# Two encoder layers on one core: the front of the first layer rebuilt

## The chip, the core and the metric

The kernel runs on one core of a Trainium2 chip. The metric is the device time of one execution in microseconds, the median over runs; three runs of the kernel before took 3671.44, 3666.75 and 3673.9 us. The core's engines are TensorE (PE; its weight loads are listed as PEld), VectorE (DVE), ScalarE (ACT), GpSimd (POOL) and SyncE (SP, which issues most DMAs). Each works through its own list of instructions in order and waits on semaphores for the others.

## What is computed

The reference is a trunk of two layers over 1024 tokens of width 1024, in float32. The first layer mixes tokens by multi-head latent attention, the second by dilated windows; both end in an MLP. Only the first layer's start matters here:

```python
cond = jax.nn.silu(c)
mod = (cond @ ada_w[i] + ada_b[i]).reshape(B, N_MOD, D)        # shift1, scale1, gate1, shift2, ...
h = rms_norm(x, norm_mix[i]) * (1 + scale1) + shift1
proj = h @ w_in                                                # 384 + 256 + 32 columns
q_lat, kv_lat = proj[..., :384], proj[..., 384:640]
k_rope = rope(proj[..., 640:], pos)
q = (rms_norm(q_lat, g_qa) @ w_qb).reshape(B, S, 16, 96)       # 64 plain + 32 rotated per head
kv = (rms_norm(kv_lat, g_kva) @ w_kvb).reshape(B, S, 16, 128)  # 64 of k, 64 of v per head
q = rms_norm(rotated q, g_q);  k = rms_norm(k with k_rope, g_k)
o = softmax(q k^T / sqrt(96)) v;  y = o @ w_o;  x = x + gate1 * y
```

The positions are an input. The second layer's bias depends on them; where they are evenly spaced (they are here) a short way to the bias table is taken, else a long one under a branch.

## The kernel before

Every large product is made of three float32r matmuls: both operands are split into a high part and the rest, and high x high, high x rest and rest x high are summed in PSUM (`mm3`, lines 289 to 293). A split (`split`, 114) is a copy on ACT and a subtraction on DVE. Tiles live in SBUF pools of 4 KB slots: `G` has 29 slots for the whole program, `X` 16 slots from `aux()` on. The instructions of each engine are ordered by a planner that simulates the program, so the order of the source is kept where nothing is won by another; an instruction passed to `keep_in_program_order` keeps its place among the others so marked.

**Start (lines 1383 to 1407).** SP loads four tiles of x, the constants (`const_loads`, 119) and the first half of the modulation weights of scale1 and shift1. `bias_check` (796) loads the positions into one partition and tests on DVE, over 1023 elements, whether they are even. `consts` (133) makes `cond`. Four tiles of x are normalised together (`xhat`, 234), transposed on PE and kept (`xT`). For each half of the 1024 columns the modulation sum is made on DVE, eight multiply-adds of 512 columns for each of the two (`ada_sum`, 167), and summed over partitions by matmuls with a column of ones (`ada_end`, 177, line 192). Then h is written, transposed, as h high and h rest (`h_store`, 262). The branch on even positions (`bias_any`, 894, line 897) follows; every engine passes it together.

**First projection (`mla`, lines 411 to 452).** Eight tiles of 128 tokens are multiplied with w_in, 384 and 288 columns, all eight blocks of D one after the other for each tile; four tiles make a half. Each tile's latents are evicted and normalised (428 to 437), after four tiles they are transposed (444). Before each tile of the second half stand two modulation steps (420). `rope_tables` (315) makes sines and cosines on POOL and DVE.

**Heads (lines 470 to 520).** For two halves of the heads and eight tiles each, q (`pq`, two banks, two buffers) and k and v (`pkv`, the same) are projected; ACT and DVE sum squares, the factor of the norm is made (`rstd`, 99), DVE multiplies q (`tq`, 502) and k (505, 507), POOL rotates q (`rope`, 376) and multiplies it by the weights of both norms (512, 514), and `st` is stored to DRAM but for the first four heads (520).

**Attention (lines 523 to 652).** 64 units, each of two blocks of 128 queries, in a software pipeline: scores, minimum (575), exp (576), factor (579), transposes (590), product with v (603). `prep` (528) transposes and splits a head's q and k; that of head 0 stands before the loop. Every eleventh of the 269 turns has a modulation step (`ada_step`, 206), which sums 128 columns of a later modulation, by turns on DVE (eight operations, 173 and 175) and on POOL (four, 162 to 165).

Of the kernel before, what the change touches and what calls it, by code (L numbers as in the profile page):

```python
# [9 lines left out]
F32 = mybir.dt.float32  # L10
# [10 lines left out]
P = 128  # L21
# [20 lines left out]
class K:  # L42
# [76 lines left out]
    def const_loads(self):  # L119
        nc, a = self.nc, self.a  # L120
        rows = self.G("rows", [P, P], F32)
        nc.sync.dma_start(out=rows[0:96, :], in_=a["ada_b"].rearrange("l (r p) -> (l r) p", p=P))
        nc.sync.dma_start(out=rows[96:112, :], in_=a["norm_mix"].rearrange("l (r p) -> (l r) p", p=P))
        nc.sync.dma_start(out=rows[112:128, :], in_=a["norm_mlp"].rearrange("l (r p) -> (l r) p", p=P))
        rows2 = self.G("rows2", [P, P], F32)
        nc.sync.dma_start(out=rows2[0:3, :], in_=a["mla_g_qa"].rearrange("o (r p) -> (o r) p", p=P))
        nc.sync.dma_start(out=rows2[3:5, :], in_=a["mla_g_kva"].rearrange("o (r p) -> (o r) p", p=P))

        cc = self.C("cc", [P, 8])
        nc.sync.dma_start(out=cc, in_=a["c"].rearrange("o (p j) -> p (o j)", j=8))  # L130
        return rows, rows2, cc
# [17 lines left out]
    def ada_load(self, l, s, c, n, alloc=None):  # L149

        w = self.a["ada_w"][l].rearrange("(p j) n -> p j n", j=8)[:, :, s * 1024 + c : s * 1024 + c + n]
        if alloc is None:
            t = self.dap.tile([P, 8, n], F32, tag="w", name=self.nm("adaw"))
            self.nc.sync.dma_start(out=t, in_=w)
            return [t]
        m = 1024 // n
        return [self.load(w[:, j : j + m, :], (P, m, n), "adaw", alloc=alloc) for j in range(0, 8, m)]

    def ada_sum_pool(self, w, n, acc):

        tt = self.nc.gpsimd.tensor_tensor
        tt(w, w, self.cond.unsqueeze(2).broadcast_to([P, 8, n]), op=ALU.mult)
        tt(w[:, 0:4], w[:, 0:4], w[:, 4:8], op=ALU.add)
        tt(w[:, 0:2], w[:, 0:2], w[:, 2:4], op=ALU.add)
        tt(acc, w[:, 0], w[:, 1], op=ALU.add)

    def ada_sum(self, ws, n, acc):
        nc = self.nc
        m = 8 // len(ws)
        for j in range(8):  # L170
# [3 lines left out]
            else:  # L174
                nc.vector.scalar_tensor_tensor(acc, g, self.cond[:, j : j + 1], acc, op0=ALU.mult, op1=ALU.add)  # L175

    def ada_end(self, l, s, c, n, acc, psp, tag):
# [10 lines left out]
        if (l, s) not in self.mods:  # L188
            self.mods[(l, s)] = self.C(f"mod{l}{s}", [P, 8])
        d0, nd = c // P, n // P  # L190
        for d in range(nd):
            nc.tensor.matmul(ps[:, d : d + 1], acc[:, d * P : (d + 1) * P], self.ones[:, 0:1], start=True, stop=True)
        mo = self.mods[(l, s)][:, d0 : d0 + nd]
        b = l * 48 + s * 8 + d0
        nc.vector.tensor_tensor(mo, ps[:, 0:nd], self.colc[:, b : b + nd], op=ALU.add)
        if s % 3 == 1:
            b = (96 if s == 1 else 112) + l * 8 + d0
            nc.vector.scalar_tensor_tensor(mo, mo, 1.0, self.colc[:, b : b + nd], op0=ALU.add, op1=ALU.mult)
# [26 lines left out]
    def xhat1(self, x, alloc=None):  # L225
# [4 lines left out]
        nc.scalar.activation(g, x, AF.Square, scale=1.0 / 32.0, accum_out=ms)  # L230
# [45 lines left out]
    def h_steps(self, xs, mods, alloc=None, halloc=None, single=False):  # L276
# [4 lines left out]
        if single:  # L281
            steps = [lambda psp, tag, x=x: xh.append(self.xhat1(x, alloc)) for x in xs]
# [12 lines left out]
    def load(self, src, shape, name, dt=F32, alloc=None):  # L295
        g = (alloc or self.G)(name, shape, dt)
        self.nc.sync.dma_start(out=g, in_=src)
# [17 lines left out]
    def rope_tables(self):  # L315
        nc, a = self.nc, self.a
        eng = nc.gpsimd
        pos = self.M("posc", [P, 8], I32)
        nc.sync.dma_start(out=pos, in_=a["positions"].rearrange("o (t p) -> p (o t)", p=P))
        posf = self.M("posf", [P, 8])  # L320
        nc.vector.tensor_copy(posf, pos)
# [54 lines left out]
    def rope(self, eng, out, x, t, n, name):  # L376

        cos = self.cs["cos"][:, t : t + 1, :].broadcast_to([P, n, 16])
        sin = self.cs["sin"][:, t : t + 1, :].broadcast_to([P, n, 16])
        u = self.mp.tile([P, n, 16], F32, tag="rp", bufs=3, name=self.nm(name + "u"))  # L380
        w = self.mp.tile([P, n, 16], F32, tag="rp", bufs=3, name=self.nm(name + "w"))
        x1, x2 = x[:, :, 0:16], x[:, :, 16:32]
        eng.tensor_tensor(u, x1, cos, op=ALU.mult)
        eng.tensor_tensor(w, x2, sin, op=ALU.mult)
        eng.tensor_tensor(out[:, :, 0:16], u, w, op=ALU.subtract)
        u = self.mp.tile([P, n, 16], F32, tag="rp", bufs=3, name=self.nm(name + "u2"))
        w = self.mp.tile([P, n, 16], F32, tag="rp", bufs=3, name=self.nm(name + "w2"))
        eng.tensor_tensor(u, x2, cos, op=ALU.mult)
        eng.tensor_tensor(w, x1, sin, op=ALU.mult)
        eng.tensor_tensor(out[:, :, 16:32], u, w, op=ALU.add)  # L390


    def mla(self, at, wi, xs1, mods, tail):
# [9 lines left out]
        def heads_w(hf, alloc):  # L403
            wq = [self.wsplit(a["mla_w_qb"][0, c * P : (c + 1) * P, hf * 768 : (hf + 1) * 768], (P, 768), "wq",
                              gain=self.colc[:, 128 + c : 129 + c], alloc=alloc) for c in range(3)]
            wkv = [self.wsplit(a["mla_w_kvb"][0, c * P : (c + 1) * P, hf * 1024 : (hf + 1) * 1024], (P, 1024), "wkv",
                               gain=self.colc[:, 131 + c : 132 + c], alloc=alloc) for c in range(2)]
            return wq, wkv

        with tc.tile_pool(name="psA", bufs=2, space=PSUM, reuse_waits="tile") as psp:  # L410
            at1, steps = self.h_steps(xs1, mods, self.X, self.X)
            steps.pop(0)(psp, "b1")
            self.rope_tables()
            for half in range(2):
                lats = []
                h = (at, at1)[half]
                for t in range(half * 4, half * 4 + 4):
                    if half == 1:
                        for i in range(2):
                            self.ada_step(psp, "b1", i == 1)  # L420
                    tl = slice((t % 4) * P, (t % 4 + 1) * P)
                    ps = psp.tile([P, 2, 512], F32, tag="b2", name=self.nm("psin"))
                    for o, n, b in ((0, 384, 0), (384, 288, 1)):
                        for d in range(ND):
                            self.mm3(ps[:, b, 0:n], h(0, d)[:, tl], h(1, d)[:, tl],
                                     wi[d][0][:, o : o + n], wi[d][1][:, o : o + n], d == 0, d == ND - 1)
                    ms = self.sm("lms", 2)
                    lat = self.G("lat", (P, 640), F32)
                    nc.scalar.activation(lat[:, 0:384], ps[:, 0, 0:384], AF.Square, scale=QL ** -0.5,
                                         accum_out=ms[:, 0:1])  # L430
                    nc.scalar.activation(lat[:, 384:640], ps[:, 1, 0:256], AF.Square, scale=KL ** -0.5,
                                         accum_out=ms[:, 1:2])
                    r = self.rstd(ms, 2, "lr")
                    nc.vector.tensor_scalar(lat[:, 0:384], ps[:, 0, 0:384], r[:, 0:1], None, op0=ALU.mult)
                    nc.vector.tensor_scalar(lat[:, 384:640], ps[:, 1, 0:256], r[:, 1:2], None, op0=ALU.mult)
                    nc.vector.tensor_copy(krw[:, t, :], ps[:, 1, 256:288])
# [1080 lines left out]
```

## Time and profile before

| | us |
|---|---|
| median of three runs | 3671.44 |
| the profiled execution | 3669.05 |
| its span | 3667.3 |
| PE busy | 3493.4 |
| DVE busy | 2458.3 |
| ACT busy | 1482.0 |
| POOL busy | 960.6 |

The span is the time from the first instruction to the last of the profiled execution. An engine's busy time leaves out waits, branches and the issuing of DMAs. A row of a group names the line, the engine, the operation, the tile written and those read, the shape and the count, then the busy time, the mean duration of one in ns, and the idle time before them with what ended it. A row of the timeline begins with its start and its duration. A row of the stages gives busy time by engine, the clock that PE was granted (1.00 is full speed), the share of the DMA engines and GB/s.

### The profile page before, as it was taken

The numbers are of one execution on the slowest core, as the hardware profiler recorded it, in microseconds if no ns is written. First come the engines' busy times: TensorE is split into PE (matmuls) and PEld (weight loads), VectorE is DVE, ScalarE is ACT, GpSimd is POOL, SyncE is SP. The second block draws the span as 40 slices with busy tenths as digits, with TensorE's granted clock in tenths as the row PEclk, the third lists the DMA queues.
The fourth block names the chain that finished last, engine by engine and source line by source line (L and its number), as shares of the span: only waits on it lengthen the run. The fifth ranks groups of instructions, "written<-read, shape, count | busy, mean of one in ns | idle before, by whom it ended". The sixth has DMA issues, their size and how long they took to land.

```text
span 3667.3 us, 58438 instructions
## 1 busy us (share of the span) xinstructions
PE 3493.4 (95%) x22163; PEld 3109.7 (85%) x22163; DVE 2458.3 (67%) x5045; ACT 1482.0 (40%) x3133; POOL 960.6 (26%) x1323
## 2 busy tenths in 40 slices
PE   3799999999999999999999999999998899999999
PEld 3787788778888878889999999999998778888887
DVE  6788888767777775566667666676877565455554
ACT  3336777653211112235556454565555232112221
POOL 3476555530111111112222222233334011111111
PEclk8899999999999999999999999999999999999999
DMA  5232222251344431133323333332334511111112
GB/s 193 84 115 64 64 75 64 64 172 48 104 122 125 132 86 48 46 103 100 99 83 94 101 105 93 107 89 85 96 93 122 141 52 46 46 46 58 47 52 63
DMA packets 355211, 323.61 MB, mean 88 GB/s; under 512 B 25478, under 2 KB 322891, under 8 KB 354924
## 3 DMA queue, kind: packets, MB, share of 16 engines
q1 hardware_dynamic: 348332, 305.13, 28.4%
q0 software_dynamic: 6592, 14.68, 1.3%
q8 instruction: 177, 2.90, 0.3%
q14 instruction: 110, 0.90, 0.1%
HBM read 260.73 MB, written 47.49 MB: 84 GB/s over the span
## 4 chain that ended last, share of the span: by engine, by line
PE 84%; DVE 7%; ACT 3%; DMA 2%; issue 1%; POOL 1%; SPq 0%; DVEq 0%; ACTq 0%; POOLq 0%
PE psy L291 8%; PE psy L292 8%; PE psy L293 8%; PE psproj L291 7%; PE psproj L293 7%; PE psproj L292 7%; PE psu L291 7%; PE psu L292 6%; PE psu L293 6%; PE pav L603 2%; PE pss L1111 2%; PE ppt L590 2%; PE pspt L1137 2%; PE psq L1080 2%; PE psav L1152 1%
## 5 line engine op out<-in xcount | busy, mean ns | idle before, releaser
L306 POOL TENSOR_TENSOR w2r<-w2r,gate 128x1024 f32<-128x1024 f32 x64 | 166.6, 2605 | 1330.0 <-DMA w2r<-in_mlp_w 1023.0
L750 DVE TENSOR_TENSOR x<-x,psy 128x1024 f32<-128x1024 f32 x256 | 310.9, 1216 | 287.1 <-PE psy L293 287.0
L291 PE MATMUL psu<-hT,w1h 128*128 128x512 f32 x1024 | 403.7, 394 | 5.8 <-ACT w1h L116 4.2
L292 PE MATMUL psu<-hT,w1h 128*128 128x512 f32 x1024 | 399.9, 391 | 0.0
L291 PE MATMUL psy<-w2h,u 128*128 128x512 f32 x1024 | 399.4, 390 | 0.0
L293 PE MATMUL psu<-hT,w1l 128*128 128x512 f32 x1024 | 399.1, 390 | 0.0
L292 PE MATMUL psy<-w2l,u 128*128 128x512 f32 x1024 | 398.9, 390 | 0.0
L293 PE MATMUL psy<-w2h,u 128*128 128x512 f32 x1024 | 398.6, 389 | 0.0
L291 PE MATMUL psproj<-wqkh,hTp 128*128 128x256 f32 x1024 | 296.8, 290 | 0.0
L293 PE MATMUL psproj<-wqkh,hTp 128*128 128x256 f32 x1024 | 291.5, 285 | 0.0
L292 PE MATMUL psproj<-wqkl,hTp 128*128 128x256 f32 x1024 | 290.0, 283 | 0.0
L737 ACT ACTIVATE relu<-psu 128x512 f32<-128x512 f32 x128 | 76.2, 596 | 525.2 <-PE psu L293 524.9
L291 PEld LDWEIGHTS psu<-hT,w1h 128*128 128x128 f32 x1024 | 192.8, 188 | 48.6 <-ACT w1h L116 4.7
L293 PEld LDWEIGHTS psu<-hT,w1l 128*128 128x128 f32 x1024 | 192.7, 188 | 40.6
L292 PEld LDWEIGHTS psy<-w2l,u 128*128 128x128 f32 x1024 | 192.3, 188 | 40.1 <-issue 0.4
L291 PEld LDWEIGHTS psy<-w2h,u 128*128 128x128 f32 x1024 | 192.2, 188 | 40.1 <-DVE x L750 0.3
L293 PEld LDWEIGHTS psy<-w2h,u 128*128 128x128 f32 x1024 | 192.2, 188 | 40.0
L292 PEld LDWEIGHTS psu<-hT,w1h 128*128 128x128 f32 x1024 | 192.9, 188 | 38.8 <-issue 0.2
L175 DVE SCALAR_TENSOR_TENSOR adacc<-adaw,cond,adacc 128x128 f32<-128x128 f32 (+1 forms) x476 | 205.0, 434 | 10.8 <-DMA adaw<-in_ada_w 1.8
L292 PEld LDWEIGHTS psproj<-wqkl,hTp 128*128 128x128 f32 x1024 | 195.8, 191 | 0.0
L293 PEld LDWEIGHTS psproj<-wqkh,hTp 128*128 128x128 f32 x1024 | 195.6, 191 | 0.0
L291 PEld LDWEIGHTS psproj<-wqkh,hTp 128*128 128x128 f32 x1024 | 195.6, 191 | 0.0
(313 smaller groups left out, 9520.7 us busy)
## 6 DMA issues: line engine op xcount, KB each, us to landing
adaw<-in_ada_w SPq DMA_DIRECT2D x96, 512.0 KB
w1r<-in_mlp_w SPq DMA_DIRECT2D x64, 512.0 KB
w2r<-in_mlp_w SPq DMA_DIRECT2D x64, 512.0 KB
bt<-bias SPq DMA_DIRECT2D x128, 256.0 KB
wqkr<-in_dil_w_in SPq DMA_DIRECT2D x96, 256.0 KB
qkv<-st SPq DMA_DIRECT2D x24, 512.0 KB
hraw<-qkv SPq DMA_DIRECT2D x24, 512.0 KB
wvr<-in_dil_w_in SPq DMA_DIRECT2D x24, 512.0 KB
```

Source lines behind the costliest of these rows:

```text
L175: nc.vector.scalar_tensor_tensor(acc, g, self.cond[:, j : j + 1], acc, op0=ALU.mult, op1=ALU.add)
L291: mm(out, lh, rh, start=first, stop=False)
L292: mm(out, lh, rl, start=False, stop=False)
L293: mm(out, ll, rh, start=False, stop=last)
L306: nc.gpsimd.tensor_tensor(raw, raw, row, op=ALU.mult)
L590: nc.tensor.transpose(pt[:, k * P : (k + 1) * P], u["p"][i][:, kt * P : (kt + 1) * P], self.ident)
L603: nc.tensor.matmul(ps[:, j % 2, :], heads[h]["v"][:, kt, :], u["pT"][hl][kt // 4][:, kt % 4, :], start=kt == 0 and hl == 0, stop=kt == 7 a ...
L737: nc.scalar.activation(r, ps, AF.Relu)
L750: nc.vector.tensor_tensor(xs[t], xs[t], ps, op=ALU.add)
L1080: nc.tensor.transpose(ps[:, (2 * e + k) * P : (2 * e + k + 1) * P], s4[:, i, e, 64 * k : 64 * k + 128], identr)
L1111: nc.tensor.matmul(ps[:, e * 256 : (e + 1) * 256], q[:, e, k, :], u["k"][:, e, w0 : w0 + 256], start=k == 0, stop=k == 1)
L1137: nc.tensor.transpose(ps[:, (n * e + b) * P : (n * e + b + 1) * P], p[:, e, c : c + P], self.ident)
```

## The change

- The constants and positions are issued from ACT's queue instead of SP's. The positions' test works on 128 partitions of eight and ends with a matmul over the partitions. The branch stands ahead of the first layer's work.
- The first modulation sums are made by PE alone: a matmul of each 128x128 block of the weights with a column of `cond`, summed in PSUM over the eight parts (`ada_pe`).
- The first half's projection runs by chunks of D (512, 256 and 256 columns of the modulation): sums, h, and then two blocks of D at a time for all four tiles, whose PSUM stays open. PE's order is marked to be kept, as are the loads, the squares and the copies of w_in's split. w_in comes in three DMAs for each block, reordered to 384, 32 and 256 columns. x is normalised tile by tile.
- The second half's projection has no modulation steps. k is rotated on POOL, four tiles at a time.
- In the heads, q goes from PSUM straight into `st` and is rotated there; the weights of both norms are applied in head preparation, as the factor of the split. POOL makes the product of 507. Head 0 is prepared ahead of the last tile, in this stage's PSUM.
- In attention every eighth turn has a modulation step, one product on POOL and one reduction on DVE.

```diff
     def ada_sum_pool(self, w, n, acc):
-        tt = self.nc.gpsimd.tensor_tensor
-        tt(w, w, self.cond.unsqueeze(2).broadcast_to([P, 8, n]), op=ALU.mult)
-        tt(w[:, 0:4], w[:, 0:4], w[:, 4:8], op=ALU.add)
-        tt(w[:, 0:2], w[:, 0:2], w[:, 2:4], op=ALU.add)
-        tt(acc, w[:, 0], w[:, 1], op=ALU.add)
+        self.nc.gpsimd.tensor_tensor(w, w, self.cond.unsqueeze(2).broadcast_to([P, 8, n]), op=ALU.mult)
+        self.nc.vector.tensor_reduce(acc, w.rearrange("p j n -> p n j"), op=ALU.add, axis=AX.X)
...
+    def ada_pe(self, l, ss, c, n, ws, psp, tag):
+        nc = self.nc
+        ps = psp.tile([P, 512], F32, tag=tag, name=self.nm("psac"))
+        nd = n // P
+        m = 1024 // n
+        for k, s in enumerate(ss):
+            for j in range(8):
+                for d in range(nd):
+                    self.pinned(nc.tensor.matmul(ps[:, k * nd + d : k * nd + d + 1],
+                                                 ws[s][j // m][:, j % m, d * P : (d + 1) * P],
+                                                 self.cond[:, j : j + 1], start=k == j == d == 0,
+                                                 stop=k == len(ss) - 1 and j == 7 and d == nd - 1))
+        for k, s in enumerate(ss):
+            self.ada_col(l, s, c, n, ps[:, k * nd : (k + 1) * nd])
+
+    def pinned(self, ins):
+        return self.tc.keep_in_program_order(ins)
...
+            chunks = [(0, 512), (512, 256), (768, 256)]
+            wi, raws, loads = [], [], [ada0]
+            for q, (c, n) in enumerate(chunks):
+                if q:
+                    loads.append({s: self.ada_load(0, s, c, n, self.X) for s in (1, 0)})
+                raws += [w_in(d) for d in range(c // P, (c + n) // P)]
+            xs1 = xs1()
...
+            for q, ds in ((0, (0, 1)), (1, (2, 3)), (2, (4, 5))):
+                w_in_split(*ds)
+                make_h(q)
+                for d in ds:
+                    for t in range(4):
+                        project(*P4[t], at, t, d)
+            w_in_split(6, 7)
+            at1, steps = self.h_steps(xs1, mods, self.X, self.X, single=True, pin=True)
+            lats = []
+            for t in range(4):
+                steps.pop(0)(psp, "b1")
+                for d in (6, 7):
+                    project(*P4[t], at, t, d)
+                if t % 2 == 1:
+                    lats += [latent(*P4[i], i) for i in (t - 1, t)]
...
+            if n == "q":
+                nc.scalar.activation(hi, pt[0:QK, :], AF.Copy, scale=gq)
+                nc.vector.scalar_tensor_tensor(lo, pt[0:QK, :], gq, hi.bitcast(F32), op0=ALU.mult, op1=ALU.subtract)
...
-                    st = [(self.X if hf == 1 or b == 0 and t < 6 else self.G)("st", (P, 4, 256), F32) for b in range(2)]
-                    tq = self.G("tq", (P, 8, QK), F32)
-                    sq = tq.rearrange("p h e -> p (h e)")
+                    st = [(self.X if hf == 0 and b == 0 else self.G)("st", (P, 4, 256), F32) for b in range(2)]
+                    sq = self.G("sq", (P, 8 * QK), F32)
...
-                        nc.vector.tensor_tensor(tq[:, 4 * b : 4 * b + 4, :], q4[:, b],
+                        nc.vector.tensor_tensor(st[b][:, :, 0:QK], q4[:, b],
...
-                        nc.vector.tensor_tensor(st[b][:, :, 160:192], rk.broadcast_to([P, 4, 32]),
+                        nc.gpsimd.tensor_tensor(st[b][:, :, 160:192], rk.broadcast_to([P, 4, 32]),
...
+                    if hf == 1 and t == 6:
+                        for k in ("q", "kv"):
+                            pt = psp.tile([P, 2, 512], F32, tag=k, name=self.nm("pqk"))
+                            for i in range(2):
+                                prep(0, (k == "kv") * 2 + i, pt[:, i, :])
...
-                if n % 11 == 5:
-                    self.ada_step(psp, "t", n % 22 == 5)
+                if n % 8 == 4:
+                    self.ada_step(psp, "t", True)
...
-        xs = [k.load(xrow(t), (P, 1024), "x") for t in range(4)]
-        cl = k.const_loads()
-        ws = {(s, 0): k.ada_load(0, s, 0, 512, k.G) for s in (1, 0)}
-        k.bias_check()
...
+            xs = [k.load(xrow(t), (P, 1024), "x") for t in range(4)]
+            ada0 = {s: k.ada_load(0, s, 0, 512, k.G) for s in (1, 0)}
+            cl = k.const_loads()
+            k.bias_check(psp)
             k.consts(cl, psp)
...
         k.bias_any()
         k.aux()
+        xh = [k.xhat1(x, k.X) for x in xs]
```

More of the change, by code (lines that the diff above doesn't have):

```diff
@@ L374, in rope_tables, with rope @@
             self.cs[name] = out
[L376 to L381, printed above, removed]
+    def rope(self, eng, out, x, cos, sin, n, name):
+        u, w, u2, w2 = (self.mp.tile([P, n, 16], F32, tag=f"rp{n}", bufs=8 if n == 4 else 4, name=self.nm(name + k))
+                        for k in ("u", "w", "u2", "w2"))
         x1, x2 = x[:, :, 0:16], x[:, :, 16:32]
@@ L384, in rope, with mla @@
         eng.tensor_tensor(w, x2, sin, op=ALU.mult)
+        eng.tensor_tensor(u2, x2, cos, op=ALU.mult)
+        eng.tensor_tensor(w2, x1, sin, op=ALU.mult)
         eng.tensor_tensor(out[:, :, 0:16], u, w, op=ALU.subtract)
[L386 to L393, printed above, removed]
+        eng.tensor_tensor(out[:, :, 16:32], u2, w2, op=ALU.add)
+    def mla(self, xh, ada0, xs1, mods, tail):
         nc, a, tc = self.nc, self.a, self.tc
@@ L630, in av @@
                         del heads[h]
-            for part in range(4):
-                prep(0, part)
             us = [unit(h, j) for h in range(H) for j in range(4)]
```

323 lines of the change are left out of this document (175 added, 148 removed).

## The prediction

> **What bounds the kernel now.** I read the page first, then the busy time of the engines stage by stage, then PE's waits and the timeline of each stage. The whole program is bound by PE; the change touches what lies before 790 us. Its stages, cut at the first projection matmul (72.07 us), the end of the first projection's first half (107.9), the first matmul of the head projections (164.4), their last (270.4), and the end of attention's first unit (302.7) and last (789.6):
>
> ```profile
> span 3667.3 us, 58438 instructions
> ...
> 0.00:72.07 72.07, 13.06 (x66) 11.48 (x67) 44.85 (x77) 23.41 (x39) 13.06 (x30) 0.83 0.64 211
> 72.07:107.90 35.83, 35.83 (x225) 35.71 (x226) 23.30 (x48) 16.14 (x43) 25.86 (x56) 0.92 0.19 70
> 107.90:164.40 56.50, 40.95 (x245) 37.14 (x244) 47.43 (x141) 16.67 (x44) 28.64 (x44) 0.87 0.34 106
> 164.40:270.40 106.00, 100.12 (x482) 87.84 (x480) 91.70 (x201) 44.02 (x97) 75.01 (x144) 0.97 0.31 109
> 270.40:302.70 32.30, 21.77 (x106) 17.37 (x107) 24.45 (x58) 14.48 (x28) 18.49 (x40) 0.84 0.31 103
> 302.70:789.60 486.90, 455.38 (x3016) 392.88 (x3015) 400.48 (x700) 348.12 (x635) 267.31 (x296) 0.99 0.24 75
> ...
> PE psac L192 <- DVE adacc L175: 17.1, 1, 17.1
> ```
>
> The columns are the stretch, its length, busy time of PE, PE's weight loads, DVE, ACT and POOL, the granted clock, the share of DMA and GB/s. PE works 13 of the first 72 us: it waits for DVE's modulation sums, 17.1 us of it at once (the row from PE's waits). In the third stage it idles 15.6 us, in the heads' stage 5.9, in the handover to attention 10.5, in attention 31.5. Everything the change can win from idle PE is in these rows; what it adds to PE is paid in full.
>
> The profiled execution took 3669.05 us, 1.75 over its span and 2.4 under the median of the three runs (3671.44). I make the sum against the execution.
>
> **First modulation sums, 0 to 107.9 us.** Removed from DVE: 32 multiply-adds of 512 columns. Added to PE: for each of 1024 columns' blocks, 2 x 8 x 8 = 128 matmuls of a 128x128 weight by one column, 64 of them (A0) before the first h, 32 each (A1, A2) between the projection's chunks, in an order fixed for PE. Old ones of the same form give the price:
>
> ```profile
> 10.06 0.17 DVE L142 TENSOR_TENSOR cond<-cc,e 128x8 f32<-128x8 f32 x1
> 11.35 0.49 DVE L173 TENSOR_SCALAR adacc<-adaw,cond 128x512 f32<-128x512 f32 x1 [1.13 <-DMA adaw<-in_ada_w]
> ...
> 44.53 1.84 PE L192 MATMUL psac<-ones,adacc 128*128 128x1 f32 x16
> 66.31 1.84 PE L192 MATMUL psac<-ones,adacc 128*128 128x1 f32 x8 [1.04 <-DVE mod L198]
> ...
> 43.90:47.30 3.40, 2.48 (x23) 1.00 1.05 402
> 74.60:78.00 3.40, 3.40 (x13) 0.50 0.99 361
> 78.00:81.40 3.40, 3.40 (x21) 0.99 0.62 247
> ```
>
> Four columns' blocks make 8 instructions, so a matmul of this form is two instructions: 0.23 us at full clock (1.84/8) and 0.46 at half (1.84/4). Which holds? The row from 43.9 is a stretch of full clock that is mostly the 16 instructions of 44.53; PE counts as busy 2.48 of 3.4 us in it, and right after it the clock is halved until 78.0. So one-column matmuls do not keep the clock up, and A0, which begins cold, has nothing else in it: 64 x 0.46 = 29.4 us. It can begin when cond (10.06) and the first weights (11.35) are there and the branch is behind; I take 12.0, bounds 10 and 25 (rival 2).
>
> [...]
>
> A1 and A2 begin warm. [...] The projection after each of A0, A1 and A2 then begins cold; from 72.07 to 78.0 it took 5.9 us to be released, I take 5.1, which costs 2.55 us each.
>
> ```profile
> L271 ACT ACTIVATE ht<-xT,mod,mod 128x512 f32<-128x512 f32 x8 | 5.9, 801 | 11.2 <-DVE mod L195 11.2
> ...
> L117 DVE TENSOR_TENSOR hT<-ht,hT 128x512 fp32r<-128x512 f32 x16 | 11.1, 714 | 0.9 <-ACT hT L116 0.9
> ...
> 40.77 3.93 PE L252 MATMUL pst<-ident,xh 128*128 128x128 f32 x20 [0.26 <-ACT xT L1395]
> ...
> 110.18 0.33 PE L293 MATMUL psin<-wih,hT 128*128 128x384 f32 x1
> 110.35 0.33 PE L291 MATMUL psin<-wih,hT 128*128 128x384 f32 x1
> ...
> 113.37 0.29 PE L291 MATMUL psin<-wih,hT 128*128 128x288 f32 x1
> 113.50 0.29 PE L292 MATMUL psin<-wil,hT 128*128 128x288 f32 x1
> ```
>
> The projection's pair of matmuls starts 0.172 + 0.131 = 0.303 us apart (rows of 110.18 and 113.37; start to start); 416 and 256 columns have the same sum as 384 and 288, so four tiles by eight d by three cost 96 x 0.303 = 29.1 us as before. Between A0 and the first of them lie two small DVE steps, the scaling on ACT (0.80), a copy and the subtraction (0.71): 3.2 us with their handoffs. The 28 transposes of x that do not fit into A0's shadow take 0.2 each cold (40.77: 3.93/20), half of that warm: 4.0 us. So the first half ends at 12.0 + 29.4 + 3.2 + 29.1 + 2 x 10.1 + 3 x 2.55 + 4.0 = 105.6 us, where it ended at 107.9: **2.3 us gained**. Hidden at no cost: 24 DMA issues for w_in instead of 8, and A1's and A2's weights, all issued on SP while PE is in A0; the constants' and positions' ten issues, which leave SP for ACT; the new first-half normalisation. Were A0 short, they would have to be weighed again.
>
> **Second half, 107.9 to 164.4.** The eight modulation steps that stood here (with their PE waits for DVE and POOL) go to attention; PE's order is fixed. What is left is 29.1 us of projection, 20 transposes of latents and 32 of x at half of 40.77's 0.2 less a little, 0.09 (4.7 us), then the tail: the last two tiles share a PSUM bank, so both are evicted after the last matmul, and transposed.
>
> ```profile
> 107.06 0.49 ACT L429 ACTIVATE lat<-psin 128x384 f32<-128x384 f32 x1 [5.36 <-PE psin L293]
> ...
> 111.13 0.47 DVE L435 TENSOR_SCALAR lat<-psin,lry 128x256 f32<-128x256 f32 x1
> ...
> 159.22 0.44 PE L444 MATMUL pslt<-ident,lat 128*128 128x128 f32 x2 [2.93 <-DVE lat L434]
> ...
> 164.40 0.67 PE L291 MATMUL pq<-wqh,latT 128*128 128x384 f32 x1
> ```
>
> One tile's eviction took 4.5 us (107.06 to 111.6); two take 6.0, since only the work of ACT and DVE adds. From the first transpose after it to the first head matmul it took 5.2 us. Sum 45.0 against 56.5: **11.5 gained**. The k rotation, 48 small DVE operations, becomes 12 on POOL beside PE's work; w_qb's and w_kvb's splits lie beside the projection.
>
> **Heads, 164.4 to 270.4.** Fourteen tiles follow each other evenly, (270.24 - 180.48)/14 = 6.41 us each. PE needs 18 x 0.172 + 12 x 0.228 = 5.83 (512 columns by the line through 288 and 384), call it 5.87.
>
> ```profile
> 180.48 0.66 PE pq L291
> ...
> 270.01 0.39 PE L293 MATMUL pkv<-wkvh,latT 128*128 128x512 f32 x1
> ...
> 198.68 0.78 DVE L507 TENSOR_TENSOR st<-hry,kr 128x128 f32<-128x128 f32 x1
> 199.38 0.55 DVE L502 TENSOR_TENSOR tq<-pq,hry 128x384 f32<-128x384 f32 x1
> 199.85 0.28 DVE L507 TENSOR_TENSOR st<-hry,kr 128x128 f32<-128x128 f32 x1
> ...
> L383 POOL TENSOR_TENSOR qru<-tq,cos 128x128 f32<-128x128 f32 x16 | 7.4, 462 | 11.1 <-DVE tq L502 11.1
> ...
> L554 POOL TENSOR_TENSOR hv<-st,hv 128x64 fp32r<-128x64 f32 x8 | 2.4, 327 | 0.0
> ```
>
> DVE works without a break here and its chain frees PSUM. L507 leaves it for POOL: 0.70 by the starts plus 0.28, so DVE's loop falls to 5.4, under PE's. POOL drops four products with the gain and gets two L507 and twelve rotations of half the size: 2 x 0.46 + 12 x 0.33 = 4.9 us a tile, if they cost what L554's 64 columns cost; at L383's 0.46 it is 6.4 and nothing is won. I take the first, as the size is L554's. Gain 14 x 0.54 = 7.5. Against it head 0's 16 transposes move here (1.5 us) and take a turn of both PSUM pairs, so the last tile waits for the last but one to be evicted: some 3.5 us. Net **2.5 gained**.
>
> **Handover.**
>
> ```profile
> 276.86 3.62 PE L548 MATMUL pqk<-ident,st 128*96 128x128 f32 x16 [5.65 <-DVE tq L502]
> 280.14 1.20 PE L291 MATMUL pss<-kh,qh 96*128 96x512 f32 x2
> ...
> 289.50 0.64 PE L291 MATMUL pss<-kh,qh 96*128 96x512 f32 x1 [4.14 <-ACT p L576]
> ```
>
> From 270.24 to the first scores at 280.14 went 9.9 us, waiting and head 0's cold transposes. With head 0 prepared, scores need only PSUM, freed some 5 us after the last tile: 4.9 won. The second stall, 4.14 us, sits where bias work entered DVE as soon as the old gain row was dead; that gain now lives through attention, so this work must come later: 4.1 won. Bounds 0 and 14; I take **9.0**.
>
> **Attention.** It carries 34 modulation steps instead of 24 (eight from the front, two from behind). For the 24, of which half were DVE's:
>
> ```profile
> 285.00:785.00 500.00, 7.64 (x46) 5.32 (x46) 38.99 (x95) 5.03 (x11) 0.99 0.23 73
> ...
> L575 DVE TENSOR_REDUCE am<-pss x128: 1193/1205/1226, 287.0 to 779.3; 128x1 f32<-128x1024 f32 x128
> ...
> L1298 ACT ACTIVATE hTp<-hT x13: 1096/1175/1194, 1983.8 to 2015.1; 128x512 fp32r<-128x512 f32 x13
> ```
>
> PE paid 7.64 us, 0.32 a step: ten more cost **3.2**. DVE paid 39.0; now every step is one POOL product and one reduction over 1024 elements, 1.2 us by L575, 34 x 1.2 = 41: no change. The reduction reads with a stride, which no DVE reduction here does; bounds 1.2 and 2.4, since a strided copy on ACT takes 1175 ns where the plain one of its size takes half. q's split with a factor keeps its two instructions: nothing.
>
> [...]
>
> **Sum.** 2.3 + 11.5 + 2.5 + 9.0 - 3.2 = 22.1 us. 3669.05 - 22.1 = 3646.9; with half of the distance to the median, 3648.
>
> **Rivals.**
> [...]
> 2. *The branch comes late.* All engines pass it together, now ahead of A0, and the position loads share the DMA engines with 6 MB of x and weights, which at the first stage's mean of 211 GB/s take 28 us. A0 from 25 instead of 12 costs 13: 3661. Against it: they are on ACT's queue, and small.
> 3. *Attention pays, slower than before.* PE idles 31.5 us there while DVE gives 39 to the steps; at that ratio, 0.8 us a us, reductions of 2.4 us (82 us) put 34 us more on PE. With the 22.1 won this is 12 lost: 3681. It decides from about 2.0 us a reduction on. Against it: not all idling there is owed to the steps. [...]
> 4. *Nothing gained in the heads*, POOL at 6.4: 3655, inside the forecast's own range.
>
> **Numbers.** Forecast (with 4) 0.5, own range 3633 to 3660; clock 0.25; branch 0.13; attention 0.12. The range reaches to the clock's time with its spread (A0's start at 10, all of the handover's 14) below and to the branch's with a missed handover above: 3613 to 3676. A change under 0.2%, 7 us, cannot be told from none (the three runs span 7): faster below 3664. From the forecast 0.47, all of the clock's, most of the branch's 0.07: 0.79 faster; 0.1 same; 0.11 slower.
>
> **What would show it.** A0: 64 matmuls from some 12 us, granted clock 0.50 to about 42 us, first projection matmul at 45. First half over near 106, first head matmul near 151, heads at 5.9 us a tile with PE waiting for nothing but the last one, first scores 5 us after. In attention the reduction at 1.2 us and PE idle near 31 us. Wrong would be: full clock in A0 (rival 1), the branch after 20 us (2), a reduction above 2 us or PE idle above 50 us in attention (3), POOL without a break in the heads (4).

## The result, and the profile after

The changed kernel takes 3719.24 us (median of 4 runs, 3715.94 to 3720.23), the kernel before in the same session 3671.85: a ratio of 1.0130, 95% interval 1.0112 to 1.0147. The forecast was 3648. The profiled execution has a span of 3716.9 us against 3667.3, so 49.6 us have to be found. The same stages as in the prediction, cut by the same events of the changed kernel (columns: stretch, length, busy PE, weight loads, DVE, ACT, POOL, granted clock, share of DMA, GB/s). One bound of the prediction's stages is a little late: in the kernel before, the first half's last matmul ends at 107.03 us and the second half's first begins at 107.66, not at 107.9.

```profile
0.00:58.80 58.80, 31.95 (x148) 30.79 (x149) 10.33 (x44) 11.94 (x25) 1.24 (x22) 1.00 0.78 264
58.80:114.57 55.77, 55.77 (x340) 55.51 (x339) 18.25 (x48) 17.28 (x37) 28.51 (x73) 0.82 0.14 41
114.57:178.56 63.99, 45.69 (x265) 40.90 (x263) 38.02 (x87) 27.75 (x76) 9.36 (x25) 0.82 0.09 27
178.56:291.90 113.34, 101.73 (x498) 92.31 (x496) 75.51 (x177) 45.40 (x101) 65.75 (x226) 0.94 0.32 111
291.90:319.00 27.10, 20.75 (x89) 16.61 (x89) 18.86 (x30) 12.57 (x25) 15.17 (x30) 0.75 0.19 62
319.00:837.70 518.70, 466.16 (x3037) 401.67 (x3035) 429.25 (x661) 354.59 (x636) 281.25 (x277) 0.97 0.25 81
837.70:3716.90 2879.20, 2825.04 (x18026) 2524.83 (x18024) 1819.17 (x3810) 1018.31 (x2249) 537.96 (x716) 0.99 0.30 86
```

| step | forecast | measured | difference |
|---|---|---|---|
| first half of the projection over | 2.3 gained | 6.7 lost (114.6 for 107.9) | 9.0 |
| second half | 11.5 gained | 7.5 lost (64.0 for 56.5) | 19.0 |
| heads | 2.5 gained | 7.3 lost (113.3 for 106.0) | 9.8 |
| handover | 9.0 gained | 5.2 gained (27.1 for 32.3) | 3.8 |
| attention | 3.2 lost | 31.8 lost (518.7 for 486.9) | 28.6 |
| the rest of the program | 0 | 1.5 lost (2879.2 for 2877.7) | 1.5 |

Together 49.6 lost where 22.1 were to be gained. Of the four steps that were to gain, only the handover did. Each stage has a place of its own where the time went.

**Front.** The timeline of DVE and of ACT's queue, and PE's groups of the changed kernel until 58 us:

```profile
6.16 0.17 DVE L903 TENSOR_TENSOR cdiff<-cpos 128x7 int32<-128x7 int32 x1 [5.12 <-DMA cpos<-in_positions]
...
14.29 0.16 DVE L903 TENSOR_TENSOR cdiff<-cpos 127x1 int32<-127x1 int32 x1 [4.87 <-DMA cpos<-in_positions]
```
```profile
1.70 0.54 ACTq L899 DMA_DIRECT2D cpos<-in_positions  x1
2.27 5.91 ACTq L900 DMA_DIRECT2D cpos<-in_positions  x1
...
14.71 0.38 ACTq L122 DMA_DIRECT2D rows<-in_ada_b  x1
...
21.07 0.24 ACTq L127 DMA_DIRECT2D rows<-in_mla_g_kva  x1
```
```profile
L184 PE MATMUL psac<-cond,adaw 128*128 128x1 f32 x128 | 27.4, 352 | 3.8 <-PEq L999 3.8
...
L144 PE MATMUL psc<-ident,rows 128*128 128x128 f32 x1 | 0.4, 447 | 7.2 <-DMA rows<-in_norm_mlp 7.2
```

A0, the first 64 modulation matmuls, takes 27.4 us (forecast 29.4) but begins at 27.45. Ten small loads went to ACT's queue. One of them, a broadcast of 8 bytes to 128 partitions, takes 5.91 us to issue. The load to 127 partitions, issued at 1.70, is used at 14.29. The constants are issued behind all this, from 14.71 to 21.07, and PE waits 7.2 us for them, because the transpose of the constants stands ahead of the branch in its queue; for the branch itself it waits another 3.8. This is the rival of the late branch. Of the 15.45 us by which A0 is late, 6.4 came back: 2.0 in A0, and 4.5 from A0's end to the end of the first half (59.7 us, where the sum had 64.2). There I had charged 5.1 us of half clock to the projection after A0, and the first clock record, at full speed, is 0.9 us after its first matmul.

**Second half.** ACT and PE about the last matmul of the first half (114.57), and below them PE of the kernel before at the same point:

```profile
103.88 1.05 ACT L253 ACTIVATE xh<-x 128x1024 f32<-128x1024 f32 x1
...
116.84 1.05 ACT L253 ACTIVATE xh<-x 128x1024 f32<-128x1024 f32 x1
...
119.43 1.05 ACT L253 ACTIVATE xh<-x 128x1024 f32<-128x1024 f32 x1
```
```profile
120.72 0.69 PE L277 MATMUL pst<-ident,xh 128*128 128x128 f32 x2 [5.71 <-DVE xh L256]
123.86 0.69 PE L277 MATMUL pst<-ident,xh 128*128 128x128 f32 x2 [2.46 <-DVE xh L256]
...
132.44 1.12 PE L277 MATMUL pst<-ident,xh 128*128 128x128 f32 x4 [0.21 <-DVE ht L298]
133.21 0.70 PE L474 MATMUL psin<-wih,hT 128*128 128x416 f32 x1
```
```profile
106.87 1.03 PE L252 MATMUL pst<-ident,xh 128*128 128x128 f32 x8
107.66 0.42 PE L291 MATMUL psin<-wih,hT 128*128 128x384 f32 x1
```

The third and fourth square of the second half's x run 13 us and more after the second: the first latents stand between them on ACT, and these wait for the last matmuls of their tiles. Only then can x be normalised and transposed, and h follows at 1.3 us a d (the steps of PE from 123.86 to 132.44 wait for DVE). PE projects again at 133.21, 18.6 us after the first half. In the kernel before, the transposes of x for the second half stand among the first half's matmuls, and the second half goes on 0.6 us after the first (107.66 after 107.03). From 133.21 on PE needs 45.4 us (to 178.56), against 42.1 of the 45.0 that I had summed, since 2.9 of these are the transposes of x, which here lie ahead.

**Heads.** ACT and PE at the first three tiles:

```profile
185.75 1.15 ACT L335 ACTIVATE wkvh<-wkvr,colc 128x1024 fp32r<-128x1024 f32 x1
190.90 0.60 ACT L618 ACTIVATE sqk<-pkv 128x512 f32<-128x512 f32 x1 [4.00 <-PE pkv L318]
...
191.65 1.15 ACT L335 ACTIVATE wkvh<-wkvr,colc 128x1024 fp32r<-128x1024 f32 x1
192.69 0.81 ACT L616 ACTIVATE sq<-pq 128x768 f32<-128x768 f32 x1
```
```profile
198.32 0.66 PE L316 MATMUL pq<-wqh,latT 128*128 128x384 f32 x1 [7.46 <-DVE st L626]
```

The square of the first tile's q (192.69) comes behind the second tile's kv (190.90) and the split of the last weight; until then nothing frees PSUM and PE stands for 7.46 us. After that the tiles follow each other every 5.91 us (eleven of them from 206.44 to 271.42), where the forecast had 5.87.

**Attention.** The groups of the new steps, and PE's waits (line waited for: us, times, longest):

```profile
L162 DVE TENSOR_REDUCE adacc<-adaw 128x128 f32<-128x1024 f32 x31 | 61.4, 1980 | 6.6 <-POOL adaw L161 6.5
```
```profile
PE ppt L683 <- DVE pT L117: 22.9, 30, 3.0
PE pav L696 <- DVE pT L117: 13.0, 13, 1.8
```

The reduction takes 1.98 us, not 1.2, and the two waits for DVE's half of p^T grow to 35.9 us. In the kernel before they were 14.1 (the rows below). Of the 31.8 us that attention loses, 21.0 are more idle time of PE and 10.8 more busy time; seven spells at half clock, 27 us together, lie in this stage where the kernel before has one of 7.

```profile
PE ppt L590 <- DVE pT L117: 8.3, 19, 1.0
...
PE pav L603 <- DVE pT L117: 5.8, 12, 1.2
```

### The profile page after: what moved, and what is told of

It is laid out like the page before. It is cut to its first block, busy times and chain, and to the rows that moved or that the text cites. A ratio compares the mean times of both kernels' runs of the same rounds, so it can differ in the third digit from the quotient of the medians.

```text
span 3716.9 us, 58795 instructions
## 1 busy us (share of the span) xinstructions
PE 3547.1 (95%) x22389; PEld 3162.6 (85%) x22389; DVE 2409.4 (65%) x4854; ACT 1487.8 (40%) x3145; POOL 939.2 (25%) x1368
## 4 chain that ended last, share of the span: by engine, by line
PE 83%; DVE 7%; ACT 3%; DMA 3%; issue 2%; POOL 1%; SPq 0%; DVEq 0%; ACTq 0%; POOLq 0%
PE psproj L316 8%; PE psproj L318 7%; PE psy L316 7%; PE psy L318 7%; PE psy L317 7%; PE psproj L317 7%; PE psu L316 6%; PE psu L318 6%; PE psu L317 6%; PE pav L696 2%; PE pss L1213 2%; DMA adaw<-in_ada_w 2%; PE pspt L1239 2%; PE psq L1182 2%; PE psin L474 2%
## 5 line engine op out<-in xcount | busy, mean ns | idle before, releaser
L672 POOL TENSOR_SCALAR p<-p,arl 128x1024 f32<-128x1024 f32 x128 | 143.3, 1120 | 201.6 <-DVE arl L671 167.2
```

Of the source, the lines that this page charges most:

```text
L672: nc.gpsimd.tensor_scalar(p, p, rl, 1.0, op0=ALU.mult, op1=ALU.mult)
```

## Experiments

The heads' part and attention's steps were run alone and single pieces of the change undone, then what this showed was mended, at last all together; the new front and projection were not run alone. Times are medians, with the ratio to the kernel before of the same session. Stages are from one profiled execution each; with the old front the second half is cut at its first matmul.

**Heads alone** (`heads_only`: before, with the heads' code of the change: q's gain in its split, `st` written directly, rotation on POOL, head 0 prepared in the heads' stage; below the lines that move buffers).

```diff
-                    w0 = heads_w(0, self.X)
+                    w0 = heads_w(0, [self.X] * 4 + [self.G])
...
-                    st = [(self.X if hf == 1 or b == 0 and t < 6 else self.G)("st", (P, 4, 256), F32) for b in range(2)]
+                    st = [(self.X if hf == 0 and b == 0 else self.G)("st", (P, 4, 256), F32) for b in range(2)]
```

> The kernel before with the heads' part of the change alone: q's weights in its split, products written straight into st, two L507 and the rotations on POOL, head 0 prepared in the heads' stage, k rotation still on DVE, front and attention's steps as before. Theory (the heads' part is sound, what went wrong is elsewhere): 5.9 us a tile where before took 6.41 (14 x 0.5 = 7 gained), handover 27 instead of 32.3 (5 gained), 1.5 paid for head 0's transposes, attention at 487 as before: about 3659 us. Rival A (the 7.46 us stall before the third tile belongs to this part, not to the front): about 3666. Rival B (attention's 31.6 us belong to this part: q's split with a factor, head 0's buffers): attention above 510 and about 3690.

3669.94 us, 0.9997 (0.9988 to 1.0007): no change, 4 us worse than rival A. The stages from the second half of the projection to attention:

```profile
109.96:173.88 63.92, 41.18 (x248) 38.00 (x246) 47.40 (x140) 17.24 (x44) 32.22 (x46) 0.80 0.35 112
173.88:287.73 113.85, 103.02 (x498) 93.60 (x496) 75.58 (x177) 45.62 (x102) 65.70 (x226) 0.92 0.31 107
287.73:311.40 23.67, 17.97 (x90) 14.26 (x91) 16.91 (x36) 12.19 (x24) 9.21 (x19) 0.86 0.20 67
311.40:794.33 482.93, 454.52 (x3019) 394.62 (x3018) 407.89 (x712) 351.61 (x635) 266.45 (x296) 0.99 0.24 76
```

The handover wins 8.6 and attention 4, but the stall of 7.46 us is here too, so it belongs to this part, and the second half of the projection, whose code is that of before, is 7.4 longer: the part reaches back into the stage ahead of it, by its buffers as `heads_fix` below shows. Rival B is out: attention is not slow.

**Attention's steps alone** (`steps_only`: before, with `if n % 8 == 4: ada_step(psp, "t", True)`, the new sum, and no steps in the projection).

> The kernel before with attention's steps of the change alone: 34 steps, each one product on POOL and one strided reduction on DVE, none in the second half of the first projection; front and heads as before. Theory (the steps are what attention lost): attention 515 to 520 us where before has 486.9, the second half some 8 us shorter than 56.5 (between 4 and 11), so 3669 + 31 - 8 = 3692 us. Rival (the loss is q's split or the heads' buffers): attention 487 to 492, the second half shorter, and about 3664.

3687.66 us, 1.0046 (1.0030 to 1.0063). The theory holds, 4 us short of its sum:

```profile
107.04:155.83 48.79, 38.17 (x236) 36.56 (x234) 32.37 (x119) 16.91 (x44) 13.12 (x30) 0.89 0.26 91
293.00:807.40 514.40, 465.14 (x3037) 392.56 (x3036) 429.67 (x651) 353.46 (x636) 277.90 (x284) 0.99 0.25 80
```

The second half wins 8 without its steps, attention loses 27.5, at the same granted clock (0.99) as before.

**The old sum on POOL** (`after_tree`).

```diff
-        self.nc.vector.tensor_reduce(acc, w.rearrange("p j n -> p n j"), op=ALU.add, axis=AX.X)
...
+        tt(w[:, 0:4], w[:, 0:4], w[:, 4:8], op=ALU.add)
+        tt(w[:, 0:2], w[:, 0:2], w[:, 2:4], op=ALU.add)
+        tt(acc, w[:, 0], w[:, 1], op=ALU.add)
```

> The changed kernel with one thing undone: each of the 34 steps sums as the kernel before did on POOL (a product and three additions, 4.5 us of POOL) and DVE does no reduction. Theory (DVE's strided reduction of 1.98 us holds up the copies that PE waits for): attention falls from 518.5 to about 490 and the time from 3719 to 3691. Rival A (the number and places of the steps, with the PE work and PSUM turn that each takes): attention stays at 510 to 518, time 3711 to 3719. Rival B (POOL, which would have 85 us more, now holds up the scaling of p): attention in between or above, POOL named in PE's waits.

3682.00 us, 1.0028 (1.0015 to 1.0041). Attention falls further than expected, below that of the kernel before, with the same 34 steps at the same places; POOL, 352 us busy, does not hold it up:

```profile
323.40:798.30 474.90, 449.57 (x3027) 394.06 (x3025) 382.39 (x623) 354.81 (x636) 351.92 (x367) 0.99 0.28 87
```

**The reduction without its stride** (`after_flat`: `w` read as 128 groups of eight neighbours; it adds other products than the modulation needs).

> The changed kernel with attention's reduction over eight neighbouring elements instead of eight that lie 512 bytes apart; it adds up other products than the modulation needs, so the values of the later stages are not the reference's, the work is the same. Theory (the stride is the price, as the forecast's upper bound of 2.4 us had it): the reduction takes 1.2 us instead of 1.98, DVE gets back 31 x 0.78 = 24 us, and at the 0.72 us a us that the sum on POOL returned (44 for 61) attention falls by 17 to about 501, the time to 3702. Rival (groups of eight cost 2 us in any order): reduction 1.9 to 2.0 us, attention 515 to 522, time 3715 to 3722.

3691.25 us, 1.0063 (1.0048 to 1.0079). The reduction's durations (least, median, greatest in ns) and attention:

```profile
L162 DVE TENSOR_REDUCE adacc<-adaw x33: 1204/1212/1221, 303.1 to 804.1; 128x128 f32<-128x1024 f32 x33
```
```profile
319.30:808.20 488.90, 456.45 (x3037) 395.42 (x3036) 405.83 (x661) 354.51 (x636) 282.74 (x281) 0.99 0.27 86
```
```profile
PE ppt L683 <- DVE pT L117: 10.4, 24, 1.2
...
PE pav L696 <- DVE pT L117: 5.4, 12, 0.7
```

The stride is the price: 1.21 against 1.98 us. My size of the effect was too small: 23 us of DVE (429.3 to 405.8) gave back 30 of attention, 1.3 us a us, where the forecast's ratio was 0.8. Some 10 of the 30 are the clock, an estimate from the spells at half clock (27 us in the change's attention, 7 here, at half speed; the granted clock of the stage is 0.97 there and 0.99 here); the other 20 are 0.85 a us. At equal clock, `steps_only` against the kernel before has 29.2 us more of DVE and 27.5 more of attention, 0.94 a us, its ten more steps on PE included. From here to the sum on POOL another 23 us of DVE (405.8 to 382.4) give 14, or 0.6 a us, but POOL has 69 us more there.

**Positions and constants first** (`after_first`: on SP's queue, ahead of weights and x; second differences in place of the broadcast load).

> The changed kernel with the position test without its broadcast load (second differences instead), positions and constants at the head of SP's queue ahead of the weights and of x. Theory (the late branch cost the front 15 us): the first modulation matmul at 13 to 16 us instead of 27.45, the first half over at about 101 instead of 114.6, and 3706 us. Rival (something else of the front is due at the same time: x or w_in, which now come after the weights, or the second half's late x): the matmuls begin early but the first half or the second gives it back, and the time stays within 5 us of 3719.

3718.78 us, 1.0123 (1.0106 to 1.0140), against 1.0130 for the change itself: the rival's time, but not for its reason. A0 does begin earlier, at 16.02:

```profile
L187 PE MATMUL psac<-cond,adaw 128*128 128x1 f32 x128 | 27.4, 352 | 6.5 <-PEq L1001 6.5
```

The test's result is there at 5.5 us instead of 15.8; for the branch itself PE now waits 6.5 us. The lead is 11.4 us at A0, 11.1 at the end of the first half (103.5), 9.7 at the first head matmul, 8.0 at the end of the heads, 4.0 at the end of attention (522.4 us long here), and nothing at the end of the program. So x and w_in did not take it back, and the late branch cost the front its 11 us; but undoing it did not shorten the program. Of the lead, 3 us went between the halves and the heads' end, 4 in handover and attention, 5 behind it. Why the last two differ was not found. This trace has 9 half-clock spells in attention, that of the change 7 (granted clock over the whole span 0.977 and 0.980), and `after_sq` below, whose attention has the same code, takes 512.3 us there: attention as the change has it moves by 10 us from kernel to kernel.

**Early squares** (`after_sq`).

```diff
  for t in range(4):
      steps.pop(0)(psp, "b1")
+ for t in range(4):
      for d in (6, 7):
          project(*P4[t], at, t, d)
```

> The changed kernel with one thing moved: the four squares of the second half's x are issued ahead of the last two d of the first half, where the third and fourth came after the first latents. Theory (these two squares, late on ACT, made the 18.6 us between the halves): the second half starts at 118 to 121 instead of 133.2 and the time is some 12 us shorter, 3707. Rival (h itself, made at 1.3 us a d by DVE, sets the start, or the X buffers): it starts at 128 or later and the time stays above 3714.

3707.45 us, 1.0100 (1.0081 to 1.0120): the time as the theory had it, and mostly by luck. The first half ends at 116.66, and the row is the stretch to the second half's first matmul:

```profile
116.66:126.64 9.98, 5.38 (x33) 3.79 (x31) 9.91 (x26) 6.36 (x19) 6.10 (x12) 0.83 0.00 0
```

The gap is 10.0 us instead of 18.6, not the 3 to 6 I expected, since DVE, busy for 9.91 of 9.98 us, now sets it by making h. The two late squares are 8.6 us of the gap; h itself is the rest, as the rival had it. But the first half ends 2.1 us later than in the change (116.66 for 114.57) and the second half needs 49.0 us from its first matmul on, for 45.4, so the heads begin only 3.0 us earlier (175.60 for 178.56). The two profiled executions differ by 8.2 us of span; 6.4 of these are attention's, whose code is the same.

**The heads' buffers as before** (`heads_fix`: `heads_only` with `w0` in X and `st` by the old rule).

> heads_only with the buffers as the kernel before had them: the fifth weight of the first heads in the X pool instead of G, st in X or G by the old rule; nothing else. Theory (the part's new use of G made the last kv weight's load wait for a buffer, and with it ACT, DVE and PE 7.46 us; and it held up the second half of the first projection): the gap before the third tile falls to about 3 us as before, the second half from 63.9 to about 57, and the time from 3670 to 3657. Rival (the gap comes from the order in which ACT takes the splits and the squares, whatever the buffers): the gap stays at 7.5 and the time above 3663.

3661.06 us, 0.9974 (0.9965 to 0.9984). Theory and rival are each half right:

```profile
109.94:168.01 58.07, 42.20 (x247) 38.11 (x246) 44.28 (x141) 16.92 (x44) 30.45 (x45) 0.86 0.36 113
168.01:279.54 111.53, 100.45 (x498) 91.29 (x496) 74.00 (x177) 45.87 (x101) 67.60 (x228) 0.95 0.32 114
```

The second half is back (58.1 for 63.9), so that was G's buffers. The stall stays at 7.46 us.

**A buffer for the first squares** (`heads_sqx`: `heads_fix` with `sq` and `st` of the first two tiles in X).

```diff
-                    st = [(self.X if hf == 1 or b == 0 and t < 6 else self.G)("st", (P, 4, 256), F32) for b in range(2)]
-                    sq = self.G("sq", (P, 8 * QK), F32)
+                    st = [(self.X if hf == 1 or b == 0 and t < 6 or t < 2 else self.G)("st", (P, 4, 256), F32) for b in range(2)]
+                    sq = (self.X if hf == 0 and t < 2 else self.G)("sq", (P, 8 * QK), F32)
```

> heads_fix with the squares and st of the first two tiles in the X pool. Theory (the first tile's square has no buffer until the second kv weight of the next heads is split, so ACT takes it only after the second tile's kv): the gap of 7.46 us before the third tile falls below 2 us, the cold clock after it goes, and the time from 3661 to 3653. Rival (DVE, with two tiles and the splits of five weights, is what the third tile waits for): a gap of 4 to 7 us stays and the time above 3657.

3656.84 us, 0.9958 (0.9945 to 0.9972). ACT now squares the first tile's q as soon as PE has it, before its kv, and PE's longest wait at these tiles is 1.5 us:

```profile
175.88 0.81 ACT L529 ACTIVATE sq<-pq 128x768 f32<-128x768 f32 x1 [2.76 <-PE pq L293]
...
178.65 0.60 ACT L531 ACTIVATE sqk<-pkv 128x512 f32<-128x512 f32 x1 [1.13 <-PE pkv L293]
```
```profile
PE pq L291 <- DVE st L539: 1.5, 1, 1.5
```

The heads' stage falls from 111.5 to 105.3; 2.4 of it are lost in the stage before (60.5 for 58.1), so the time falls by 4 and not by 8. The order on ACT was made by the want of a buffer, taken in G behind the weights of the next heads. That it was that of `sq`, which the square writes, and not that of `st`, which moved with it, fits the rows; the two were not moved one by one.

**All that was found, in both kernels.** `best_b` is `heads_fix` with 34 steps in attention, summed on POOL; `best_a` is the changed kernel with four changes: positions and constants first, early squares, the buffers of `heads_fix` (not those of `heads_sqx`) and the sum on POOL; `best_d` is `best_b` with the buffers of `heads_sqx`.

> heads_fix with all of the modulation steps in attention (34, none in the second half of the first projection), each summed by the old product and three additions on POOL. Theory (POOL has room and DVE is what attention waits for): second half 49 us as in steps_only, attention 475 as in after_tree, heads and handover as in heads_fix: 3657 - 8 - 8 = 3641 us. Rival (attention in after_tree was short by its different start, or the late start of the second half hid other work): attention 483 and about 3650.

> The changed kernel with all that has been named undone at once: positions and constants first, the four squares early, the old buffers of the heads, and the old sum on POOL. Theory (the losses are these four and add): 3719 - 37 (sum, as after_tree) - 12 (squares) - 7 (buffers) - 4 to 10 (branch) = 3653 to 3659. Rival (the front's parts hide each other): 3665 to 3675.

> best_b with the same two buffers moved. By the theory of heads_sqx 3646 - 8 = 3638 us; if its rival holds, above 3642. Faster than the kernel before by 0.8 to 1.0% in the one case, 0.65% in the other.

`best_b` took 3646.31 us, 0.9936 (0.9919 to 0.9952), 5 us above its sum. `best_a` took 3655.36, 0.9962 (0.9948 to 0.9976), inside its range, 64 us below the change, but not by the parts of its sum. Of 61.9 us of span, attention gives 44.1, the first half 11.6, the second 7.8, the handover 3.9; the heads give nothing (113.3 for 113.3, with the stall of 7.5 us still there), and 5.5 are lost behind attention. `best_d` took 3639.67, 0.9915 (0.9902 to 0.9929), faster than both kernels. Its stages:

```profile
0.00:106.24 106.24, 47.67 (x290) 45.08 (x291) 68.20 (x117) 39.06 (x81) 45.79 (x92) 0.87 0.49 167
106.24:155.45 49.21, 38.58 (x235) 36.90 (x234) 30.93 (x119) 16.92 (x44) 13.14 (x30) 0.90 0.26 90
155.45:259.21 103.76, 98.65 (x498) 89.48 (x496) 73.72 (x177) 45.78 (x101) 66.57 (x226) 0.98 0.32 112
259.21:281.60 22.39, 17.19 (x88) 14.01 (x89) 14.86 (x28) 12.57 (x24) 9.61 (x19) 0.85 0.14 48
281.60:757.28 475.68, 451.45 (x3037) 396.82 (x3035) 380.54 (x629) 353.61 (x635) 348.58 (x373) 0.99 0.27 86
```

It keeps the old front. The new one, mended, reaches the first head matmul at 159.2 in `best_a` where the old one is there at 154.4 in `best_b`. The first half is not the reason: with 47 us of PE in its 256 matmul instructions for the modulation it is over at 103.0, with the old one at 104.5. But the second half's first matmul comes at 112.3, 9.3 us later, and with the old front after 0.6, at 105.2: PE still waits for h.

## Why the prediction was wrong

- **Attention (28.6 of the 71.7 us).** The step that failed is the duration of one reduction, "1.2 us by L575", between bounds of 1.2 and 2.4; it measured 1.98. I had taken the nearest row by size and engine; ACT's strided copy, at twice the plain one (1175 ns against 595 to 630 in the kernel before), was the nearer one in what mattered. With 1.21 us attention takes 488.9, where the forecast had 490.1; that is close in part by luck, for the heads' part alone takes attention from 486.9 to 482.9, a gain that the forecast did not have. The third rival had the mechanism and the point from which it decides (2.0). That its price (34) is near the 31.8 measured is luck: it was for reductions of 2.4 us, and at 1.98 the rival's own ratio gives 23.
- **Second half (19.0).** PE's own work came near the sum (45.4 for 42.1). What failed is the sentence "what is left is" that work: I counted only what PE does and left out that h of the second half must be there first. Its making takes DVE 1.3 us a d and needs x's four squares, two of which were queued behind the latents. In the kernel before, this chain ran beside the first half's projection, and 0.6 us lay between the projection matmuls of the two halves; in the new order it is 18.6. Of the 11.5 us forecast, taking the steps away is worth 8 by itself (`steps_only`).
- **Heads (9.8).** The rate of a tile was right (5.91 for 5.87), the POOL rotation too, and `best_d` runs the stage in 103.8 where the forecast came to 103.5. The step left out is what the buffers do: two kinds of tile changed pools, and the first tile's square had to wait for a place in G, which held PE up for 7.46 us. I treated buffers as free. This is shown with the old front (`heads_fix`, `heads_sqx`); in the changed kernel the square's buffer was not moved, and `best_a` keeps the stall.
- **Front (9.0).** A0's length (27.4 for 29.4) and A1, A2 (10.7 and 10.4 for 10.1) held; the start, "I take 12.0, bounds 10 and 25", was 27.45, above its bound. The ten issues that I called hidden were the ones PE waited for. The second rival had it; what I held against it ("on ACT's queue, and small") was wrong. The late start of 15.45 us shows as 9.0 only because A0 and the cold projections (half clock for at most 0.9, 1.4 and 1.9 us after their first matmuls, where 5.1 was charged) had been charged too much. The 10.1 us that the sum has for each of A1 and A2 is a term that no run shows; the trace of the changed kernel has 10.7 and 10.4, with the full clock ending 3.3 us into A1 and 3.6 into A2 and half clock from there on.
- **Handover (3.8).** First scores come 4.54 us after the heads, as forecast; with the old front the stage takes 22.5 to 23.7 us (`heads_fix`, `heads_only`), where the forecast had 23.3. In the changed kernel it takes 27.1 at a granted clock of 0.75, in `best_a` 23.2 at 0.93, with PE busy 2.8 us less: the 3.8 us fit the lower clock. What lowered it was not tried.
- **The clock.** What was given 0.25 did not come: A0 ran at half rate from end to end, 0.214 us an instruction.

Two of the losses, attention's and the front's, had been named as rivals, at chances of 0.12 and 0.13. The other two had not been thought of: both are chains on other engines that PE's own sum does not show. The range of 3613 to 3676 came from one thing, or two, going wrong at a time, and its upper end left out even the third rival's 3681; here four went wrong together. Open stay why the 11 us of an earlier front do not reach the end of the program (`after_first`), and why attention with the same code differs by 10 us between kernels.

## To carry to other kernels

When work is taken off PE's path, sum the chain that feeds the next matmul as well as PE's own work, engine by engine in queue order: what was hidden behind the old work becomes the wait. A tile that changes its pool can change the order of the work on the engines that write it, here ACT's squares. And the price of another microsecond on an engine off the path is not one figure: in this attention it was 0.6, 0.94 and 1.3 us of time per us of DVE, with POOL and the clock changing too; how much of the spread is DVE's alone was not shown. Last, undo one fault at a time before adding the gains: here the earlier branch gave nothing and the early squares 3 us, where their traces promised 11 and 8.6.

## What the runs showed of the hardware

- Matmuls of one column, each with a weight load of 128x128, ran at half rate without a break for 27 us: A0 needs 27.4 us for 128 instructions, 0.214 each. A1, after the projection, shows both speeds:

```profile
L184 PE MATMUL psac<-cond,adaw 128*128 128x1 f32 x32 | 3.9, 254 | 0.0
```
```profile
L184 PE MATMUL psac<-cond,adaw 128*128 128x1 f32 x33 | 7.2, 352 | 0.0
```

  The first row is the 3.7 us from 66.6, the second the 6.9 us from 70.4: 0.116 and 0.21 us an instruction (the mean durations of the rows overlap), at a granted clock of 0.94 and 0.50. The mean of A0's rows, 352 ns, is that of the second. PE was busy all the time (27.55 of the 27.60 us from 27.4). What would have released the clock there, no run shows.
- The granted clock reads 1.00 for the first stage of the changed kernel although A0's matmuls run at half rate (0.214 us an instruction). The first clock record of this trace is at 59.7 us, and what lies before it is counted as full; there the durations decide.
- A DVE reduction of 1024 elements a partition into 128 sums takes 1.21 us over neighbours and 1.98 over elements 512 bytes apart.
- A load that broadcasts 8 bytes to 128 partitions took 5.91 us to issue, where the other small loads of the same queue took 0.24 to 0.54. Whether the broadcast or the queue's state made it so was not tried.
